# Gate products of a recurrence as three float32r products of high and low parts, in seven of eight blocks

## The chip, the cores and the metric

The kernel runs on one core of a Trainium2 chip. The metric is the device time of one launch in microseconds (us). The program is one long order of instructions on five engines: TensorE (PE, with its weight loads shown apart as PEld), VectorE (DVE), ScalarE (ACT), GpSimd (POOL) and SyncE (SP). Each engine works through its own list strictly in the order in which the program was written, and waits at an instruction until what that instruction needs is there.

## What is computed

Two layers of a transformer-like block. The change lies in layer 0, in its token mixer, a recurrence that runs over the sequence in both directions. For each of 8 blocks of 128 channels, and for each of two directions d, two gates are computed from the convolved input by 128 x 128 matrices, and the scan follows:

```python
r = sigmoid(einsum('blnc,ncd->blnd', xb, wa) + ba)
i = sigmoid(einsum('blnc,ncd->blnd', xb, wi) + bi)
log_a = -RG_C * r * softplus(-lam)
a = exp(log_a)
b = sqrt(-expm1(2.0 * log_a)) * i * xs
a_cum, h = associative_scan(combine, (a, b), axis=1)
```

After the recurrence come its output product, a mixture of experts (32 experts, whose weights stream from HBM), and layer 1 with attention and a second mixture of experts.

## The kernel before

The tokens lie on the free axis: 512 latent tokens, 2 columns of zeros and 256 context tokens, 770 columns (TL), with 128 channels on the partitions. The recurrence runs as a loop over n = 0 to 7 ("block n"). The scheduler is off: every engine does its instructions in the order in which the Python code writes them. In a block:

- TensorE computes zx (`in_mm`, L454: 24 pairs of a 512-column and a 258-column float32r product), then a unit of another, unrelated product (`unit`, L337, named adam), then zg (again 24 pairs), a second unit, the four gate products zr (L1488, plain float32, one for each gate ai and direction d) with a unit behind each direction, and goes on to zx of the next block. Blocks 6 and 7 have no units. zx and zg of block 0 are made before the loop.
- ScalarE copies zx out of PSUM into cb (L1438), applies GELU to zg (L1462, L1463), makes tanh of the four zr (L1490), and then exp, tanh and the square root (L1497 to L1501) for the scan.
- VectorE makes the convolution xc from cb (L1442, L1444), then splits the weights of the next zx into high and low parts (`half_split(0)`, L446 and L447, tile wsx), then does direction 0 of the scan of the block before (`one(0)`, L1398 to L1404), splits the weights of the next zg (`half_split(1)`, tile wsg), does direction 1 of that scan (`one(1)`, L1398 to L1407), and after GpSimd has added both directions (L1410) multiplies the sum with the GELU (L1411, tile yt). The scan of block n is thus done while TensorE is in block n + 1: the list `pend` carries it over.

A float32r product of a and b to nearly float32 accuracy is written in this kernel as three products, high*high, high*low and low*high; `in_mm` does so already. A cast to the type FR gives the high part, and a subtraction the low part.

Of the kernel before, what the change touches and what calls it, by code (L numbers as in the profile page):

```python
# [10 lines left out]
F32 = mybir.dt.float32  # L11
FR = mybir.dt.float32r
BF = mybir.dt.bfloat16
I32 = mybir.dt.int32
AF = mybir.ActivationFunctionType
# [6 lines left out]
P = 128  # L22
D = 1024
KD = D // P
SEQ = 512
CTX = 256
TL = SEQ + 2 + CTX
# [111 lines left out]
def hybrid_kernel(ctx: ExitStack, tc: tile.TileContext, A, out):  # L139
    nc = tc.nc  # L140
    ctx.enter_context(tc.manual_schedule())
    V, SC, PE, GP, SY = nc.vector, nc.scalar, nc.tensor, nc.gpsimd, nc.sync
# [129 lines left out]
    for l in range(2):  # L272
        c_ = cp.tile([P, NEXP], F32, name=f"caps{l}")
        cap = plans[l][1]
        a = 0
        while a < NEXP:
# [4 lines left out]
            a = b  # L281
# [147 lines left out]
    mx = ExitStack()  # L429
    hp = mx.enter_context(tc.tile_pool(name="hp", bufs=1, side="right"))  # L430
    hh = hp.tile([P, KD, TL], FR, name="hh")
    hl = hp.tile([P, KD, TL], FR, name="hl")
# [30 lines left out]
    def tr_tile(nm):  # L463
        return lambda: psa.tile([P, 4, P], F32, tag="tr", name=f"adat{nm}")
# [905 lines left out]
    def y_at(i, a, b):  # L1370
        return yhl[i, a // 2048][:, a % 2048:(b - 1) % 2048 + 1]
# [5 lines left out]
    def y_split(k):  # L1377
        a, b = k * TOK0, (k + 1) * TOK0
        m = min(b, (a // 2048 + 1) * 2048)
        for u, v in ((a, m), (m, b)):  # L1380
            if u < v:
                src = yt_[:, k, u - a:v - a]
                V.tensor_copy(y_at(0, u, v), src)
                V.tensor_sub(y_at(1, u, v), src, y_at(0, u, v).bitcast(F32))

    if True:
        cbs = [mp.tile([P, TL + 3], F32, name=f"cb{i}") for i in range(2)]
        for cb in cbs:
            V.memset(cb[:, 0:2], 0.0)
            V.memset(cb[:, TL + 2:TL + 3], 0.0)  # L1390

        def scans(n, xc, ge, tr, ti, av):

            hs = []

            def one(d):
                a, bb = av[d], tr[d]
                V.scalar_tensor_tensor(ti[d], ti[d], 1.0, xc, op0=OP.add, op1=OP.mult)  # L1398
                V.scalar_tensor_tensor(bb, a, 1.0, bb, op0=OP.add, op1=OP.mult)
                V.scalar_tensor_tensor(bb, bb, 0.5, ti[d], op0=OP.mult, op1=OP.mult)  # L1400
                h = mp.tile([P, SEQ + CTX], F32, tag=f"h{d}", name=f"h{n}_{d}")
                if d == 0:
                    V.tensor_tensor_scan(h[:, SEQ:], a[:, C0:TL], bb[:, C0:TL], 0.0, op0=OP.mult, op1=OP.add)
                    V.tensor_tensor_scan(h[:, 0:SEQ], a[:, 0:SEQ], bb[:, 0:SEQ], h[:, SEQ + CTX - 1:SEQ + CTX], op0=OP.mult, op1=OP.add)  # L1404
                else:
                    V.tensor_tensor_scan(h[:, SEQ:][:, ::-1], a[:, C0:TL][:, ::-1], bb[:, C0:TL][:, ::-1], 0.0, op0=OP.mult, op1=OP.add)
                    V.tensor_tensor_scan(h[:, 0:SEQ][:, ::-1], a[:, 0:SEQ][:, ::-1], bb[:, 0:SEQ][:, ::-1], h[:, SEQ:SEQ + 1], op0=OP.mult, op1=OP.add)  # L1407
                hs.append(h)

            return [lambda: one(0), lambda: one(1), lambda: (V if n == KD - 1 else GP).tensor_add(hs[0], hs[0], hs[1]),  # L1410
                    lambda: V.tensor_mul(yt_[:, n, :], ge, hs[0])]  # L1411

        def half_split(c):

            if split_n[c] % 2 == 0:
                win[c] = S.take()
            w, wi = win[c]
            r = split(w, split_n[c] % 2, f"{'xg'[c]}{split_n[c]}")
            if split_n[c] % 2:
                S.done(wi)  # L1420
            split_n[c] += 1
            return r

        rgws = [load_rgw(0)]
        pend = [lambda: None]
        for n in range(KD):
            i, b = divmod(n, 2)
            cols = None
            if b == 0 and i:
                cols = ada_end(*ada_in_mix[i - 1], aps, *side, tr_tile(f"m{i}"))  # L1430
            if b == 0 and i < 3:
                side = ada_side(*ada_in_mix[i])
            if n + 1 < KD:
                rgws.append(load_rgw(n + 1))
            rgw = rgws[n]
            cb = cbs[n % 2]
            zx = in_mm(*sx, f"x{n}") if n else z0[0]
            SC.activation(cb[:, 2:TL + 2], zx[:, 0:TL], AF.Copy)  # L1438
            if cols:
                cols()  # L1440
            xc = mp.tile([P, TL], F32, tag="xc", name=f"xc{n}", bufs=2)
            V.tensor_scalar(xc, cb[:, 0:TL], prc[:, n:n + 1], prc[:, 32 + n:33 + n], op0=OP.mult, op1=OP.add)  # L1442
            for j in range(1, 4):
                V.scalar_tensor_tensor(xc, cb[:, j:j + TL], prc[:, j * 8 + n:j * 8 + n + 1], xc, op0=OP.mult, op1=OP.add)  # L1444

            if b == 0 and i < 3:
                aps = psa.tile([P, 512], F32, tag="ada", name=f"adam{i}")

            def unit(j):
                if i < 3:  # L1450
                    ada_mm(aps, 4 * b + j)

            unit(0)
            if n + 1 < KD:
                nx = half_split(0)
            else:
                pj = Proj(0, psz, y_cut(0), y_cut(1))
                pj.split(0, ringW, "rw0", SC, GP)
                pend.pop(0)()
            zg = in_mm(*sg, f"g{n}") if n else z0[1]  # L1460
            ge = mp.tile([P, SEQ + CTX], F32, tag="ge", name=f"ge{n}", bufs=2)
            SC.activation(ge[:, 0:SEQ], zg[:, 0:SEQ], AF.Gelu_apprx_tanh)  # L1462
            SC.activation(ge[:, SEQ:], zg[:, C0:TL], AF.Gelu_apprx_tanh)  # L1463
            if n + 1 < KD:
                pend.pop(0)()
                sx, sg = nx, half_split(1)
                while pend:
                    pend.pop(0)()
            else:
                pj.split(1, ringW, "rw0", SC, GP)  # L1470

                mx.close()
                ringE = early.enter_context(tc.tile_pool(name="ringE0", bufs=RE[0], side="right"))
                ph = ExitStack()
                wp = ph.enter_context(tc.tile_pool(name="wp0", bufs=1, side="right"))
                yhl = {(u, c): ringE.tile([P, 2048], FR, tag="re0", name=f"y{'hl'[u]}{c}") for c in (2, 1, 0) for u in range(2)}
                rc, load, shares, shifted, spread = router_consts(0, wp)
                load()
                gate00 = rows_of(0, wp, 0, 1, 0, "gate")
                for k in range(3):  # L1480
                    y_split(k)
            unit(1)
            tr, ti = [], []
            for d in range(2):
                for ai in range(2):
                    z = psz.tile([P, 1024], F32, tag="z", name=f"zr{n}_{d}{ai}")
                    for a, c in ((0, SEQ), (SEQ, TL)):
                        PE.matmul(z[:, a:c], lhsT=rgw[:, ai, d, :], rhs=xc[:, a:c], start=True, stop=True)  # L1488
                    r = mp.tile([P, TL], F32, tag=f"r{ai}{d}", name=f"r{n}_{ai}{d}", bufs=2)
                    SC.activation(r, z[:, 0:TL], AF.Tanh, scale=0.5, bias=hb[:, (ai * 2 + d) * 8 + n:(ai * 2 + d) * 8 + n + 1])  # L1490
                    (ti if ai else tr).append(r)
                unit(2 + d)
            av = []
            for d in range(2):
                a = mp.tile([P, TL], F32, tag=f"a{d}", name=f"a{n}_{d}")
                cidx = d * 8 + n
                SC.activation(a, tr[d], AF.Exp, scale=spm4[:, cidx:cidx + 1], bias=spm4[:, cidx:cidx + 1])  # L1497
                SC.activation(tr[d], tr[d], AF.Tanh, scale=sp2[:, cidx:cidx + 1], bias=sp2[:, cidx:cidx + 1])
                av.append(a)
            for d in range(2):  # L1500
                SC.activation(tr[d], tr[d], AF.Sqrt)  # L1501
            pend += scans(n, xc, ge, tr, ti, av)
# [68 lines left out]
    def part(k):  # L1571
# [5 lines left out]
    side = {  # L1577
        1: lambda: (pre.add(0), pre.square(0, g0)),
        2: lambda: (pre.add(1), pre.half(0, 0)),
        3: lambda: (pre.add(2), part(4), pre.half(0, 1)),  # L1580
        4: lambda: (pre.square(1, g0), pre.mm(0)),
        5: lambda: (pre.square(2, g0), part(3), pre.half(1, 0)),
        6: lambda: (pre.half(1, 1), pre.rstd_a(g0)),
        7: lambda: (pre.rstd_b(g0), pre.norm(0, GP)),
        8: lambda: (part(2), pre.mm(1), pre.half(2, 0)),
# [289 lines left out]
    with tc.tile_pool(name="sp", bufs=1, side="right") as sp_, tc.tile_pool(name="ps", bufs=1, space=PSUM) as pss:  # L1875
# [77 lines left out]
        n = len(units)  # L1953
# [31 lines left out]
    with ExitStack() as ph:  # L1985
# [18 lines left out]
        for k in range(4):  # L2004
# [3 lines left out]
            for t in range(4):  # L2008
                pj.mm(k, t, k == 0, False)
        side = {3: lambda: (pre.gate(3), pre.add(3), pre.square(3, g0)),  # L2010
                4: lambda: shares(psa),
                5: lambda: shifted(),
                6: lambda: spread(psa),
                7: lambda: (pre.gate(0), pre.half(3, 0), pre.add(0), pre.square(0, g0)),
                8: lambda: pre.half(3, 1),
                9: lambda: pre.mm(3),
                10: lambda: pre.half(0, 0),
                11: lambda: (pre.gate(1), pre.half(0, 1), pre.add(1), pre.rstd_a(g0), pre.square(1, g1)),
# [81 lines left out]
```

## Time and profile before

| | |
|---|---|
| median of 3 runs | 1751.87 us (1751.58 to 1751.91) |
| profiled execution, its own time | 1748.35 us |
| its span, first to last instruction | 1746.6 us |
| mean granted TensorE clock | 0.95 |
| loop of the recurrence in the trace | about 66 to 259 us |

The profiled execution is 3.5 us faster than the median, and 1.75 us of its time lie outside its span. In the rows below, "idle before" stands in brackets with what ended it, and rows of the timeline merge neighbours of one line (x8 is eight records). A float32 product appears as two records. A granted clock of 1.00 is 2.4 GHz, 0.50 is 1.2 GHz.

### The profile page before, as it was taken

Reading aid. Unit: us, or ns where it says so; the run is one execution under the profiler, and the core shown is the slowest. Engines: PE = TensorE matmul, PEld = TensorE weight load, DVE = VectorE, ACT = ScalarE, POOL = GpSimd, SP = SyncE. Lnnn points to the kernel's source line nnn. Section 1 sums busy time; section 2 is a strip of 40 time slices with the busy share of each in tenths; the row PEclk is TensorE's granted clock in tenths of the full one; section 3 lists DMA queues with packets and bytes.
Section 4 is the critical chain, followed back from the end, with each engine's and each line's share of the span. In section 5 each row is a group of like instructions: output and inputs, shape, how many; then the busy total and the mean of one; then the engine's idle time right before and its main releaser. Section 6 shows DMA issues by size and latency. Waiting matters only on the chain. (4 is left out here: it accounts for less than half of the span.)

```text
span 1746.6 us, 21397 instructions
## 1 busy us (share of the span) xinstructions
PE 1529.5 (88%) x8096; PEld 774.9 (44%) x8097; DVE 828.0 (47%) x1561; ACT 415.8 (24%) x715; POOL 157.0 (9%) x300
## 2 busy tenths in 40 slices
PE   4999997858899999999788997999499999998877
PEld 1667676742333333333225666777233332432222
DVE  4586779473223224555336557864533333332213
ACT  4545562210000000100005426852110101010000
POOL 0000023231000000111002010011200000000000
PEclk9899999968999999999998998999599999999989
DMA  9565611668999999999993580036499999999996
GB/s 354 210 201 192 244 56 28 225 261 347 362 386 422 422 375 419 419 420 419 420 408 137 217 302 1 1 90 233 181 407 405 413 420 419 420 420 420 420 420 247
DMA packets 100256, 530.99 MB, mean 304 GB/s; under 512 B 10056, under 2 KB 22480, under 8 KB 45872
## 3 DMA queue, kind: packets, MB, share of 16 engines
q1 hardware_dynamic: 85600, 482.43, 69.2%
q0 software_dynamic: 10224, 36.09, 5.8%
q10 hardware_dynamic: 4320, 11.01, 1.8%
q8 instruction: 66, 1.08, 0.3%
q14 instruction: 46, 0.38, 0.1%
HBM read 516.38 MB, written 13.11 MB: 303 GB/s over the span
## 5 line engine op out<-in xcount | busy, mean ns | idle before, releaser
L1021 PE MATMUL G<-w,XT0p 128*32 128x512 f32 (+2 forms) x1312 | 262.2, 603 | 7.9 <-DMA w<-in_moe_w_up_dram 5.0
L1021 PE MATMUL Y<-w,fhs 128*32 128x512 f32 (+2 forms) x1280 | 231.6, 632 | 19.6 <-DMA w<-in_moe_w_down_dram 13.9
L1021 PE MATMUL G<-w,XT1p 128*32 128x512 f32 (+2 forms) x1376 | 230.0, 609 | 15.7 <-DMA w<-in_moe_w_gate_dram 8.0
L1021 PEld LDWEIGHTS G<-w,XT0p 128*32 128x32 f32 (+2 forms) x1312 | 75.6, 128 | 156.0 <-issue 136.8
L1021 PEld LDWEIGHTS Y<-w,fhs 128*32 128x32 f32 (+2 forms) x1280 | 67.4, 127 | 156.8 <-issue 116.8
L1021 PEld LDWEIGHTS G<-w,XT1p 128*32 128x32 f32 (+2 forms) x1376 | 58.6, 119 | 143.1 <-issue 108.1
L1099 DVE TENSOR_TENSOR xs<-xs,cm1p 128x512 f32<-128x512 f32 x112 | 73.4, 684 | 100.7 <-PE cm1p L1097 100.6
L730 POOL DMA_INDIRECT X<-hfd,ix x31 | 30.1, 971 | 661.8 <-PE xt1p L992 294.0
L1099 DVE TENSOR_TENSOR xs<-xs,cm0p 128x512 f32<-128x512 f32 x96 | 63.0, 683 | 42.6 <-PE cm0p L1097 42.0
L1091 ACT ACTIVATE yh<-yt 128x512 fp32r<-128x512 f32 x44 | 27.7, 630 | 225.4 <-DVE yt L1090 225.0
L1044 ACT ACTIVATE ft<-G 128x512 f32<-128x512 f32 x31 | 18.5, 598 | 252.4 <-PE G L1021 252.4
L1090 DVE SCALAR_TENSOR_TENSOR yt<-Y,wn,gf 128x512 f32<-128x512 f32 x28 | 21.0, 751 | 110.3 <-PE Y L1021 105.6
L583 PE MATMUL o<-pw,yh 128*128 128x512 f32 x192 | 65.1, 419 | 7.9 <-DVE pw L571 3.8
L1045 DVE SCALAR_TENSOR_TENSOR ft<-ft,G 128x512 f32<-128x512 f32 x31 | 21.3, 688 | 104.5 <-ACT ft L1044 104.5
L1054 ACT ACTIVATE fhs<-hp 128x512 f32<-128x512 f32 x31 | 18.5, 597 | 186.1 <-PE hp L1053 186.1
L454 PE MATMUL zx<-hh,wsx 128*128 128x512 f32 (+1 forms) x256 | 60.6, 349 | 1.9 <-DVE hh L415 1.8
L454 PE MATMUL zg<-hh,wsg 128*128 128x512 f32 (+1 forms) x256 | 59.2, 344 | 0.0
L1097 PE MATMUL cm1p<-yh,C 128*128 128x512 f32 x112 | 52.5, 469 | 0.6 <-ACT yh L1091 0.4
L1097 PE MATMUL cm0p<-yh,C 128*128 128x512 f32 x96 | 44.6, 464 | 5.7 <-DVE xs L1099 5.0
L1048 DVE SCALAR_TENSOR_TENSOR fh<-ft,G 128x512 f32<-128x512 f32 x31 | 21.3, 687 | 56.4 <-PE G L1021 55.5
L454 PEld LDWEIGHTS zx<-hh,wsx 128*128 128x128 f32 x256 | 40.8, 193 | 13.4 <-issue 5.0
L1488 PE MATMUL zr<-xc,rgw 128*128 128x258 f32 (+1 forms) x128 | 44.9, 496 | 0.9 <-issue 0.9
(428 smaller groups left out, 2482.4 us busy)
## 6 DMA issues: line engine op xcount, KB each, us to landing
w<-in_moe_w_gate_dram SPq DMA_DIRECT2D x128, 1024.0 KB, 16.9
w<-in_moe_w_up_dram SPq DMA_DIRECT2D x128, 1024.0 KB, 17.7
w<-in_moe_w_down_dram SPq DMA_DIRECT2D x128, 1024.0 KB, 19.1
w<-in_ada_w_dram SPq DMA_DIRECT2D x48, 1024.0 KB, 7.0
w<-in_rg_w_in_dram SPq DMA_DIRECT2D x8, 1024.0 KB, 8.2
w<-in_at_w_qkv_dram SPq DMA_DIRECT2D x6, 1024.0 KB, 10.3
kept<-yk ACTq DMA_DIRECT2D x18, 256.0 KB, 7.8
w<-in_rg_w_out_dram SPq DMA_DIRECT2D x4, 1024.0 KB, 4.8
```

Source lines behind the costliest of these rows:

```text
L454: PE.matmul(z[:, a:c], lhsT=lw[:, k, :], rhs=rh[:, k, a:c], start=(k == 0 and i == 0), stop=(k == KD - 1 and i == 2))
L583: PE.matmul(out, lhsT=a(k, t), rhs=b[:, c], start=(start and i == 0), stop=(stop and i == 2))
L730: GP.indirect_dma_start(out=X[0:n, :], out_offset=None, in_=hfd, in_offset=bass.IndirectOffsetOnAxis(ap=idx, axis=0))
L1021: PE.matmul(out[g][a:a + m], lhsT=lhs[:, k, a:a + m], rhs=w[:, at_:at_ + 512], start=(k == 0), stop=(k == last), **at)
L1044: SC.activation(t[0:n], g, AF.Tanh, scale=0.5)
L1045: V.scalar_tensor_tensor(t[0:n], t[0:n], 1.0, g, op0=OP.add, op1=OP.mult)
L1048: (first_half, lambda: V.scalar_tensor_tensor(h_[0:n], t[0:n], 0.5, u, op0=OP.mult, op1=OP.mult)))
L1090: V.scalar_tensor_tensor(yt[0:n], Y[0:n], w[0:n], g[0:n], op0=OP.mult, op1=OP.mult)
L1091: SC.activation(yh_[0:n], yt[0:n], AF.Copy)
L1097: PE.matmul(cm, lhsT=C[0:n, t * P:(t + 1) * P], rhs=y[0:n], start=(i == 0), stop=(i == 1))
L1099: V.tensor_add(a, a, cm)
L1488: PE.matmul(z[:, a:c], lhsT=rgw[:, ai, d, :], rhs=xc[:, a:c], start=True, stop=True)
```

## The change

In blocks 0 to 6 the gate products are no longer one float32 product each. ScalarE copies the gate weights rgw and the convolved input xc to float32r (gh and xh, the high parts). VectorE makes the low part xl of the input right behind the convolution, and the low part gl of the gate weights apart for each direction, at the place in the code where the gate products stand. TensorE then does gh*xh, gh*xl and gl*xh for each half of the columns. Block 7 keeps the float32 product.

```diff
+    rgp = mx.enter_context(tc.tile_pool(name="rgp", bufs=1, side="right"))
...
+            pairs = [(rgw, xc)]
+            if n + 1 < KD:
+                xh, xl = [rgp.tile([P, TL], FR, tag=f"xc{x}", name=f"xc{x}{n}") for x in "hl"]
+                gh = rgp.tile([P, 2, 2, P], FR, tag="rgh", name=f"rgh{n}")
+                SC.activation(gh, rgw, AF.Copy)
+                SC.activation(xh, xc, AF.Copy)
+                V.tensor_sub(xl, xc, xh.bitcast(F32))
+                pairs = [(gh, xh), (gh, xl)]
+
             if b == 0 and i < 3:
...
             unit(1)
             tr, ti = [], []
             for d in range(2):
+                lows = []
+                if len(pairs) > 1:
+                    gl = rgp.tile([P, 2, 1, P], FR, tag="rgl", name=f"rgl{n}{d}")
+                    V.tensor_sub(gl[:, :, 0, :], rgw[:, :, d, :], gh[:, :, d, :].bitcast(F32))
+                    lows = [gl]
                 for ai in range(2):
                     z = psz.tile([P, 1024], F32, tag="z", name=f"zr{n}_{d}{ai}")
                     for a, c in ((0, SEQ), (SEQ, TL)):
-                        PE.matmul(z[:, a:c], lhsT=rgw[:, ai, d, :], rhs=xc[:, a:c], start=True, stop=True)
+                        for u, (lw, rh) in enumerate(pairs):
+                            PE.matmul(z[:, a:c], lhsT=lw[:, ai, d, :], rhs=rh[:, a:c], start=(u == 0), stop=(u + 1 == len(pairs) and not lows))
+                        for gl in lows:
+                            PE.matmul(z[:, a:c], lhsT=gl[:, ai, 0, :], rhs=xh[:, a:c], start=False, stop=True)
```

On TensorE, in block 1, the gate products of direction 0 stood like this before, between two units (adam); zr_00 and zr_01 are the two gates of direction 0:

```order
L337 MATMUL adam_593<-w_637,cl 32x512 x4
L1488 MATMUL zr_00_809<-xc_716,rgw_584 128x512
L1488 MATMUL zr_00_809<-xc_716,rgw_584 128x258
L1488 MATMUL zr_01_814<-xc_716,rgw_584 128x512
L1488 MATMUL zr_01_814<-xc_716,rgw_584 128x258
L337 MATMUL adam_593<-w_653,cl 32x512 x4
```

and with the change like this (xch and xcl are xh and xl, rgh and rgl are gh and gl):

```order
L337 MATMUL adam_602<-w_656,cl 32x512 x4
L1504 MATMUL zr_00_846<-xch_750,rgh_752 128x512
L1504 MATMUL zr_00_846<-xcl_751,rgh_752 128x512
L1506 MATMUL zr_00_846<-xch_750,rgl_844 128x512
L1504 MATMUL zr_00_846<-xch_750,rgh_752 128x258
L1504 MATMUL zr_00_846<-xcl_751,rgh_752 128x258
L1506 MATMUL zr_00_846<-xch_750,rgl_844 128x258
L1504 MATMUL zr_01_855<-xch_750,rgh_752 128x512
L1504 MATMUL zr_01_855<-xcl_751,rgh_752 128x512
L1506 MATMUL zr_01_855<-xch_750,rgl_844 128x512
```

The first product that reads a low part of the weights (rgl) is now the third, and no product behind it can pass it.

On VectorE, the end of block 1 was before: direction 1 of the scan of block 0, the product with the GELU (L1411), and then the work of block 2:

```order
L1400 SCALAR_TENSOR_TENSOR r_01_642<-r_01_642,r_11_647 128x770
L1406 SCALAR_TENSOR_TENSOR h_1_798<-a_1_658,r_01_642 128x256
L1407 SCALAR_TENSOR_TENSOR h_1_798<-a_1_658,h_1_798,r_01_642 128x512
L1411 TENSOR_TENSOR yt__68<-ge_607,h_0_787 128x768
L344 TENSOR_TENSOR adab_579<-adam_593,adab_579 128x512
L363 COPY modc_918<-adatm_913 128x8 x2
L1442 TENSOR_SCALAR xc_921<-cb_570,prc 128x770
```

and is with the change (every line after the inserted ones has a higher number):

```order
L1401 SCALAR_TENSOR_TENSOR r_01_667<-r_01_667,r_11_676 128x770
L1407 SCALAR_TENSOR_TENSOR h_1_833<-a_1_687,r_01_667 128x256
L1408 SCALAR_TENSOR_TENSOR h_1_833<-a_1_687,h_1_833,r_01_667 128x512
L1412 TENSOR_TENSOR yt__68<-ge_616,h_0_822 128x768
L1498 TENSOR_TENSOR rgl_844<-rgw_587,rgh_752 128x256
L1498 TENSOR_TENSOR rgl_870<-rgw_587,rgh_752 128x256
L344 TENSOR_TENSOR adab_582<-adam_602,adab_582 128x512
L363 COPY modc_973<-adatm_968 128x8 x2
L1443 TENSOR_SCALAR xc_976<-cb_573,prc 128x770
L1445 SCALAR_TENSOR_TENSOR xc_976<-cb_573,prc,xc_976 128x770 x3
L1453 TENSOR_TENSOR xcl_982<-xc_976,xch_981 128x770
```

The low parts of the gate weights (rgl) of block 1 stand behind the whole scan of block 0, and the low part of the input (xcl) directly behind the convolution. On ScalarE the start of block 2 is now:

```order
L1439 ACTIVATE cb_573<-zx_918 128x770
L1451 ACTIVATE rgh_983<-rgw_692 128x512
L1452 ACTIVATE xch_981<-xc_976 128x770
L1472 ACT_TABLE_LOAD
L1472 ACTIVATE ge_1050<-zg_1001 128x512
```

where the two copies in the middle are new; the table load and the GELU followed the copy to cb directly before.

## Rows read from the trace of the kernel before

**Rows 1.** The page, parts 1 and 2: busy time; transfer rate in 40 slices.

```profile
PE 1529.5 (88%) x8096; PEld 774.9 (44%) x8097; DVE 828.0 (47%) x1561; ACT 415.8 (24%) x715; POOL 157.0 (9%) x300
...
GB/s 354 210 201 192 244 56 28 225 261 347 362 386 422 422 375 419 419 420 419 420 408 137 217 302 1 1 90 233 181 407 405 413 420 419 420 420 420 420 420 247
```

**Rows 2.** Table of stretches: block 1, and the time behind the loop.

```profile
core 0: us, PE busy (x) PEld busy (x) DVE busy (x) ACT busy (x) POOL busy (x), PEclk, DMA share, GB/s
...
78.00:105.00 27.00, 27.00 (x149) 18.40 (x145) 16.89 (x22) 14.80 (x18) 0.00 (x0) 1.00 0.70 243
...
262.00:300.00 38.00, 31.28 (x154) 24.41 (x152) 36.96 (x40) 10.30 (x11) 10.92 (x5) 0.96 0.07 15
```

**Rows 3.** Timeline of TensorE, block 1: start us, length us, instruction.

```profile
78.01 0.61 PE L454 MATMUL zx<-hh,wsx 128*128 128x512 f32 x2
...
96.39 1.07 PE L337 MATMUL adam<-w,cl 128*32 128x512 f32 x8
97.39 2.85 PE L1488 MATMUL zr<-xc,rgw 128*128 128x512 f32 x8
...
104.94 0.61 PE L454 MATMUL zx<-hh,wsx 128*128 128x512 f32 x2
```

**Rows 4.** Timeline of ScalarE, block 1.

```profile
86.81 0.81 ACT L1438 ACTIVATE cb<-zx 128x770 f32<-128x770 f32 x1 [0.49 <-PE zx L454]
```

**Rows 5.** Timeline of VectorE, block 1: convolution, and end of the chain.

```profile
87.66 0.68 DVE L1442 TENSOR_SCALAR xc<-cb,prc 128x770 f32<-128x770 f32 x1 [13.03 <-ACT cb L1438]
88.37 3.13 DVE L1444 SCALAR_TENSOR_TENSOR xc<-cb,prc,xc 128x770 f32<-128x770 f32 x3
91.42 0.42 DVE L446 CAST wsx<-w 128x512 fp32r<-128x512 f32 x1
...
107.27 0.96 DVE L1411 TENSOR_TENSOR yt__68<-ge,h 128x768 f32<-128x768 f32 x1 [1.97 <-POOL h L1410]
108.15 0.68 DVE L344 TENSOR_TENSOR adab<-adam,adab 128x512 f32<-128x512 f32 x1
```

**Rows 6.** Timeline of block 0: the last weight split on VectorE.

```profile
73.94 0.69 DVE L447 TENSOR_TENSOR wsg<-w,wsg 128x512 fp32r<-128x512 f32 x1
```

**Rows 7.** Timeline of TensorE: gate products of blocks 6 and 7, zg of 7.

```profile
231.11 5.33 PE L1488 MATMUL zr<-xc,rgw 128*128 128x512 f32 x16
236.09 0.70 PE L454 MATMUL zx<-hh,wsx 128*128 128x512 f32 x2
...
244.79 0.52 PE L454 MATMUL zg<-hh,wsg 128*128 128x512 f32 x2
...
253.32 5.33 PE L1488 MATMUL zr<-xc,rgw 128*128 128x512 f32 x16
```

**Rows 8.** Groups by line and shape, 0 to 420 us: busy us, mean ns.

```profile
L1438 ACT ACTIVATE cb<-zx 128x770 f32<-128x770 f32 x8 | 6.5, 810 | 7.8 <-PE zx L454 7.8
...
L416 DVE TENSOR_TENSOR hl<-nth,hh 128x256 fp32r<-128x256 f32 x8 | 3.4, 426 | 0.3
```

**Rows 9.** Table of stretches around idle times of TensorE, columns as in Rows 2.

```profile
41.00:43.00 2.00, 0.00 (x0) 0.00 (x0) 1.93 (x6) 0.00 (x0) 0.00 (x0) 1.00 1.01 414
44.00:46.00 2.00, 1.11 (x4) 0.71 (x4) 0.74 (x5) 0.03 (x1) 0.00 (x0) 0.50 1.00 418
47.00:50.00 3.00, 2.56 (x7) 1.90 (x8) 2.86 (x8) 2.74 (x5) 0.00 (x0) 0.50 1.03 313
50.00:53.00 3.00, 3.00 (x11) 2.54 (x11) 2.90 (x7) 1.35 (x3) 0.00 (x0) 0.50 0.33 86
54.00:57.00 3.00, 3.00 (x18) 2.51 (x18) 2.90 (x8) 2.27 (x4) 0.00 (x0) 1.00 0.00 0
269.00:272.00 3.00, 0.50 (x1) 0.19 (x1) 2.97 (x3) 2.95 (x3) 1.87 (x1) 1.00 0.01 3
272.00:275.00 3.00, 2.99 (x7) 2.41 (x8) 2.97 (x5) 1.63 (x3) 0.89 (x1) 0.50 0.00 0
276.00:279.00 3.00, 3.00 (x15) 2.47 (x14) 2.58 (x3) 1.06 (x1) 1.15 (x1) 1.00 0.00 0
287.00:290.00 3.00, 0.60 (x4) 0.29 (x2) 2.93 (x7) 0.00 (x0) 0.00 (x0) 1.00 0.00 0
```

## The prediction

> **What bounds the kernel now.** I read the page first. TensorE is busy for 88% of the span, twice as long as any other engine [rows 1], so a change in its work counts directly if the stage is its own. The table of stretches says whether it is: in block 1 of the recurrence TensorE is busy for 27.00 of 27 us, VectorE for 16.9, ScalarE for 14.8, at a granted clock of 1.00 [rows 2]. So in this loop TensorE sets the pace, and the others wait for it. Then I read the timeline of a single block, engine by engine, because the new instructions go to all three. A block of TensorE is 26.9 us, from zx at 78.01 to the next zx at 104.94, and the gate products begin at 97.39 [rows 3]. VectorE's list of the same block begins when cb is copied at 86.81 [rows 4] and ends when the instruction behind the product with the GELU starts, at 108.15 [rows 5]. The reader should see the overlap: VectorE's list ends 10.8 us after TensorE has begun the gate products, and 3.2 us after it has left them. That costs nothing now, since nothing that TensorE needs stands at the end of that list.
>
> **The change, part by part.** *Fewer passes on TensorE.* Four float32 gate products take 236.09 - 231.11 = 4.98 us where nothing stands between them [rows 7]. A float32r pair of 512 and 258 columns is what zg is made of: 24 pairs from 244.79 to 253.32, 0.355 us each [rows 7]. The new block has 12 of them, 4.27 us, so 0.71 us less per block and 5.0 us in seven blocks. The Trainium skill (FP8 and Floating Point Precision, section TensorE Precision Notes) counts true float32 as four passes and reduced float32 as one; an estimate by that count is a quarter of the 4.98 us saved, 1.25 us a block. The trace shows less, because a pair has its own cost beside the columns; by the page's count the time predicted below would be nearly 4 us lower.
>
> *The two copies on ScalarE.* The copy of the gate weights waits only for a transfer made a block earlier. The copy of xc takes 0.81 us, by the copy of the same 770 columns to cb [rows 8]; from the square root or a table function it could be 1.0. Both lie in ScalarE's idle time before the GELU. But VectorE's xl stands directly behind xc and waits for that copy.
>
> *xl on VectorE.* A subtraction of this width occupies 0.88 us until the next starts, like the product with the GELU (107.27 to 108.15) [rows 5]. In block 1 the convolution ends at 88.37 + 3.13 = 91.50, where the next instruction had started at 91.42 [rows 5]. Now the copy runs from 91.55 to 92.36, xl starts at 92.41, and the weight split at 93.29: the rest of the list is 1.87 us later.
>
> *gl on VectorE, the part that decides.* The order puts gl behind the scan of the block before and the product with the GELU. TensorE needs it at its third product. With the list moved by 1.87 us, gl starts at 108.15 + 1.87 = 110.02, takes 0.43 us by the subtraction of 256 columns [rows 8], and with 0.05 us for the signal TensorE goes on at 110.50. It came to the gate products at 97.39 and did two 512-column products, 0.47 us (2 x 512/770 of a pair). So it stands idle for about 12.6 us, and behind the waiting product stand all the other gate products, the units and zx of the next block, for which cb and the whole next list of VectorE wait. This idle time isn't hidden by anything: the chain closes on itself.
>
> *The new block.* From zx to cb 86.81 - 78.01 = 8.80 us, from cb to gl 23.69 (110.50 - 86.81), then the rest: 4.27 - 0.47 = 3.80 us of gate products and two units of 1.00 us (96.39 to 97.39) [rows 3]. Together 38.3 us, against 26.9. The second gl reuses the buffer of the first, so it waits for direction 0, but a unit of 1.00 us covers its 0.48 us. Blocks 1 to 5 are of this kind: 5 x 38.3 = 191.5. Block 6 has no units: 36.3 us. Together 227.8 us from zx of block 1 to zx of block 7, where the trace has 236.09 - 78.01 = 158.1: **69.7 us more**. Block 0 has no scan before it: gl stands behind two weight splits, the last of which starts at 73.94 [rows 6] and gives way after 0.61 us, so gl is there at 74.55 + 1.87 + 0.48 = 76.9 (xl some 4.4 us before it: two splits of a 0.42 us and a 0.69 us step, twice each [rows 5, 6]), and zx of block 1 at 76.9 + 5.8 = 82.7 instead of 78.0: **4.7 us more**. Block 7 is unchanged.
>
> *The clock.* After TensorE's idle time from 41 us on, the clock is 0.50 at 44 and still 0.50 from 47 to 53, and 1.00 from 54; after that at 270 it is 0.50 from 272 to 275 and 1.00 from 276 [rows 9]. So after each of the two TensorE ran at 1.2 GHz for 3 to 7 us of work, and lost half of that, 1.5 to 3.5 us. Each of the seven new waits is longer than these. I take 2.4 us each, the middle, **16.8 us** in all; the bounds are 10.5 and 24.5. In the loop this loss is on the path, since the rest of the gate products and zx are what VectorE waits for. The Trainium skill (TensorE: Matmul & The Clock Gate, section HAM oscillation) says that such waits between bursts put the clock down again every time, not once; the two stretches here agree, and a wait of about 2.4 us at 287 us did not do it [rows 9].
>
> *Behind the loop.* The rest moves as a whole. The weights of the experts can't use the time: from 262 to 300 us the DMA share is 0.07 [rows 2], the buffers are full, and the next ones come free by the program's steps after the loop.
>
> *The sum.* 69.7 + 4.7 + 16.8 = 91.2 us; the 5.0 us of fewer passes are in it. From the profiled execution 1748.35 + 91.2 = 1839.6; the median lies 3.5 us above that execution, so for the runs 1751.87 + 91.2 = **1843 us**.
>
> **Rivals.** *Same wait, no loss of clock*: 74.4 us, 1826 us. For it speaks that a short wait at 287 us left the clock at 1.00 [rows 9]; against it that all waits but block 0's (4.4 us) are about 12 us. *The clock stays down longer*, through the units and into zx, because the work after a wait is broken up: up to 5 us lost per wait, 35 in all, 1861 us. For it the 6 to 7 us after 47, where the first products came with gaps; against it the quick return at 276. *A slower copy and a slower list on VectorE* (1.0 us for the copy, contention): 0.3 to 0.5 us per block, 2 to 4 us, inside the range. *The other side: absorbed behind the loop.* If the time of the end were set by the transfer of expert weights, and these ran on during the waits, only the 5.0 us gained on TensorE would be seen: 1747 us. It decides if 91 us of transfers (about 38 MB at the 420 GB/s of the late slices [rows 1]) found buffers in the loop; a DMA share of 0.07 right behind it says that not even a few do [rows 2].
>
> **How the numbers follow.** Forecast as above, 0.78 (1833 to 1854, from the copy's and the clock's bounds); no loss of clock 0.10 (1824 to 1833); longer at the low clock 0.09 (1854 to 1870); absorbed 0.02 (1747); something between 0.01. A measurement of this kernel tells a change from none at about 0.2%, 3.5 us. Faster is the absorbed case, 0.02; the same 0.01; slower 0.97. The forecast's own range leaves out more than 2 in 10, so I reach into both neighbours, from 1828 to 1860.
>
> **What would show it.** In the profile after: a wait of TensorE for VectorE's gl, seven times, one of about 4.4 us and six of about 12 to 14; blocks of 38 to 42 us; a granted clock of 0.50 behind each wait; VectorE's list from cb to gl 23.7 us long without idle time except for the copy and GpSimd's sum; the float32r pairs at 0.355 us at full clock; and the time from the loop's end to the end of the program unchanged. The prediction is wrong if VectorE reaches gl earlier than TensorE, if the waits are much shorter than 12 us, or if the part behind the loop becomes shorter.

## The result: 5.2% slower, by seven waits for a small subtraction

| | before | after |
|---|---|---|
| median of the runs | 1751.72 us (1748.58 to 1751.91, 4 runs) | 1840.89 us (1840.04 to 1845.18, 4 runs) |
| profiled execution, its own time | 1748.35 us | 1840.04 us |
| its span | 1746.6 us | 1838.3 us |
| mean granted TensorE clock | 0.950 | 0.925 |

The time grew to 1.0522 of before, interval 1.0505 to 1.0539: 89 us by the medians, 91.7 us between the two profiled executions. 1843 us had been forecast, with a difference of 91.2 us.

The page of the kernel after, part 1, answers to [rows 1]:

```profile
PE 1542.3 (84%) x8152; PEld 790.5 (43%) x8153; DVE 841.9 (46%) x1582; ACT 425.2 (23%) x729; POOL 155.8 (8%) x300
```

TensorE's busy time grew by only 12.8 us, so nearly all of the loss is time in which TensorE did nothing. The table of waits, TensorE alone, from 60 to 350 us of the kernel after, says for whom it waited (us in total, times, longest):

```profile
PE zr L1506 <- DVE rgl L1498: 79.5, 7, 14.3
PE zr L1504 <- ACT xch L1452: 1.7, 1, 1.7
PE zr L1504 <- DVE xcl L1453: 0.5, 1, 0.5
```

rgl is the low part of the gate weights (gl in the code): seven waits, one for each changed block, 79.5 us. TensorE's timeline of blocks 0, 1 and 6 shows where each stands, and answers to [rows 3] and [rows 7]:

```profile
77.08 0.79 PE L1506 MATMUL zr<-xch,rgl 128*128 128x512 f32 x1 [4.09 <-DVE rgl L1498]
84.88 0.61 PE L454 MATMUL zx<-hh,wsx 128*128 128x512 f32 x2
...
104.27 0.50 PE L1504 MATMUL zr<-xch,rgh 128*128 128x512 f32 x1
104.61 0.40 PE L1504 MATMUL zr<-xcl,rgh 128*128 128x512 f32 x1
117.34 0.79 PE L1506 MATMUL zr<-xch,rgl 128*128 128x512 f32 x1 [12.34 <-DVE rgl L1498]
...
125.47 0.61 PE L454 MATMUL zx<-hh,wsx 128*128 128x512 f32 x2
...
321.55 0.79 PE L1506 MATMUL zr<-xch,rgl 128*128 128x512 f32 x1 [14.33 <-DVE rgl L1498]
327.70 0.51 PE L454 MATMUL zx<-hh,wsx 128*128 128x512 f32 x2
```

In block 1 two products run, and the third, the first to read rgl, comes 12.34 us later. From zx to zx this block takes 125.47 - 84.88 = 40.6 us, against 26.9. The record behind the wait is 0.79 us long; the same 512-column product, when it isn't the first, takes 0.40 us at full clock.

VectorE's timeline of the same block says why rgl is late, and answers to [rows 5]:

```profile
94.54 0.68 DVE L1443 TENSOR_SCALAR xc<-cb,prc 128x770 f32<-128x770 f32 x1 [13.63 <-ACT cb L1439]
95.26 3.13 DVE L1445 SCALAR_TENSOR_TENSOR xc<-cb,prc,xc 128x770 f32<-128x770 f32 x3
99.31 0.96 DVE L1453 TENSOR_TENSOR xcl<-xc,xch 128x770 fp32r<-128x770 f32 x1 [0.92 <-ACT xch L1452]
...
115.99 0.96 DVE L1412 TENSOR_TENSOR yt__68<-ge,h 128x768 f32<-128x768 f32 x1 [1.92 <-POOL h L1411]
116.87 0.42 DVE L1498 TENSOR_TENSOR rgl<-rgw,rgh 128x256 fp32r<-128x256 f32 x1
120.74 0.43 DVE L1498 TENSOR_TENSOR rgl<-rgw,rgh 128x256 fp32r<-128x256 f32 x1 [3.46 <-PE zr L1506]
```

The subtraction is 0.42 us of work. It stands behind the two weight splits and the scan of the block before (from 100.19, where xl gives way, to about 114.1), GpSimd's sum, and the product with the GELU. And the list itself begins only when cb is there (the wait of 13.63 us), which comes from TensorE's zx: so each engine waits for the other once a block. ScalarE's cb starts at 93.70, and TensorE goes on at 117.34, 23.64 us later.

The table of stretches, columns as in [rows 2], shows all of block 1, its part behind the wait, and the time behind the loop:

```profile
85.00:125.00 40.00, 27.66 (x152) 20.27 (x152) 19.88 (x26) 15.55 (x18) 1.80 (x1) 0.83 0.32 107
...
118.00:119.50 1.50, 1.50 (x7) 1.31 (x6) 0.00 (x0) 0.69 (x1) 0.00 (x0) 0.50 0.00 0
120.00:122.00 2.00, 2.00 (x12) 0.60 (x10) 0.43 (x1) 0.90 (x1) 0.00 (x0) 0.55 0.00 0
122.00:125.00 3.00, 3.00 (x24) 2.05 (x20) 0.00 (x0) 1.33 (x2) 0.00 (x0) 1.00 0.57 150
...
345.00:385.00 40.00, 33.62 (x150) 24.77 (x149) 38.94 (x42) 16.77 (x19) 16.92 (x11) 0.91 0.08 17
```

TensorE is busy for 27.7 of 40 us, where it had been busy all the time; behind the wait the granted clock is 0.50 to about 122 us, that is 1.2 GHz for some 4.5 us, and 1.00 again from there. Behind the loop nothing was caught up: from zx of block 7 (327.70) to the profiled execution's end it is 1512.3 us, and it was 1512.3 before (1748.35 - 236.09 [rows 7]). That the two agree so closely is chance: from the start of o, behind the loop, to its end, a profiled execution takes between 1483.5 and 1492.5 us in the ten kernels of this document.

### The profile page after: what moved, and what is told of

Its sections match the earlier page's. It is cut to its first block, busy times and chain, and to the rows that moved or that the text cites. A ratio compares the mean times of both kernels' runs of the same rounds, so it can differ in the third digit from the quotient of the medians.

```text
span 1838.3 us, 21550 instructions
## 1 busy us (share of the span) xinstructions
PE 1542.3 (84%) x8152; PEld 790.5 (43%) x8153; DVE 841.9 (46%) x1582; ACT 425.2 (23%) x729; POOL 155.8 (8%) x300
## 5 line engine op out<-in xcount | busy, mean ns | idle before, releaser
L1506 PE MATMUL zr<-xch,rgl 128*128 128x512 f32 (+1 forms) x56 | 25.6, 457 | 79.5 <-DVE rgl L1498 79.5
L1091 ACT ACTIVATE yh<-yt 128x512 fp32r<-128x512 f32 x44 | 27.7, 630 | 228.0 <-DVE yt L1090 221.3
L1508 ACT ACTIVATE r<-zr,hb 128x770 f32<-128x770 f32 x32 | 28.9, 904 | 114.3 <-PE zr L1506 113.0
L1506 PEld LDWEIGHTS zr<-xch,rgl 128*128 128x128 f32 x56 | 14.5, 258 | 84.0 <-DVE rgl L1498 82.8
L1097 PE MATMUL cm0p<-yh,C 128*128 128x512 f32 x96 | 44.6, 464 | 5.8 <-DVE xs L1099 5.1
## 6 DMA issues: line engine op xcount, KB each, us to landing
w<-in_moe_w_gate_dram SPq DMA_DIRECT2D x128, 1024.0 KB, 19.8
```

The costliest lines, as they stand in the source:

```text
L1091: SC.activation(yh_[0:n], yt[0:n], AF.Copy)
L1097: PE.matmul(cm, lhsT=C[0:n, t * P:(t + 1) * P], rhs=y[0:n], start=(i == 0), stop=(i == 1))
L1506: PE.matmul(z[:, a:c], lhsT=gl[:, ai, 0, :], rhs=xh[:, a:c], start=False, stop=True)
```

## Experiments

Two questions: is the place of gl on VectorE the whole cause, or do the new copies, subtractions and products cost something themselves; and what part is the clock? All kernels start from the changed one, and each is compared with runs of the kernel before on the same chip.

**1. gl early, in all seven blocks.** Both low parts of the weights are made right behind xl, each in a buffer of its own. The space for the second buffer comes from two small temporaries that are reused.

```diff
-        spm4 = cp.tile([P, 16], F32, name="spm4")
-        sp2 = cp.tile([P, 16], F32, name="sp2")
+        spm4, sp2 = sb_, sq_
...
+            def low(d):
+                gl = rgp.tile([P, 2, 1, P], FR, tag=f"rgl{d}", name=f"rgl{n}{d}")
+                V.tensor_sub(gl[:, :, 0, :], rgw[:, :, d, :], gh[:, :, d, :].bitcast(F32))
+                return [gl]
+
+            gls = [low(d) if len(pairs) > 1 else [] for d in range(2)]
...
-                lows = []
-                if len(pairs) > 1:
-                    gl = rgp.tile([P, 2, 1, P], FR, tag="rgl", name=f"rgl{n}{d}")
-                    V.tensor_sub(gl[:, :, 0, :], rgw[:, :, d, :], gh[:, :, d, :].bitcast(F32))
-                    lows = [gl]
+                lows = gls[d]
```

> The two subtractions that make the low parts of the gate weights stand directly behind the low part of the input on VectorE, each into a buffer of its own; everything else is as in the changed kernel. If the place of these subtractions is the cause: no wait of TensorE for them in blocks 1 to 6, 12 pairs of 0.355 us in place of 4.98 us there (0.71 us less per block, 4.3 us), block 0 about 0.8 us longer (its products wait for the copy and two subtractions), so about 1748 us. If the float32r products, the switch between kinds of product, or the added copies and subtractions themselves cost the time, it stays above 1760 us.

Measured: 1749.65 us (1744.41 to 1754.71, 12 runs), before 1749.03 (24 runs), ratio 1.0002 (0.9989 to 1.0015). No wait for rgl is left in the table of waits. So the place of a 0.42 us instruction is the whole loss of 89 us: the same copies, subtractions and products, with gl some 20 instructions earlier, cost nothing in sum. But neither is the gain of some 5 us from fewer passes seen. In the loop it is there: TensorE's timeline of this kernel has

```profile
77.91 0.61 PE L454 MATMUL zx<-hh,wsx 128*128 128x512 f32 x2
...
97.87 0.39 PE L1508 MATMUL zr<-xch,rgl 128*128 128x512 f32 x1
...
103.90 0.61 PE L454 MATMUL zx<-hh,wsx 128*128 128x512 f32 x2
...
226.29 0.39 PE L1506 MATMUL zr<-xch,rgh 128*128 128x512 f32 x1
...
230.50 0.52 PE L454 MATMUL zx<-hh,wsx 128*128 128x512 f32 x2
...
250.33 7.11 PE L1506 MATMUL zr<-xc,rgw 128*128 128x512 f32 x16 [2.68 <-ACT pw L567]
257.77 0.70 PE L582 MATMUL o<-pw,yh 128*128 128x512 f32 x2 [0.33 <-DVE yh L1382]
```

The kernel before has, on ScalarE and on TensorE, for the copy to cb of block 7 and for the first product behind the loop (o, the output product of the recurrence):

```profile
245.81 0.79 ACT L1438 ACTIVATE cb<-zx 128x770 f32<-128x770 f32 x1
```

```profile
259.80 0.70 PE L583 MATMUL o<-pw,yh 128*128 128x512 f32 x2 [1.15 <-DVE yh L1383]
```

From zx of block 1 to zx of block 7 it is 152.6 us, against 158.1 [rows 3, 7]: 5.5 us less. Then block 7 gives most of it back. Its gate products (still float32) come 19.8 us behind its zx, where before they came 253.32 - 236.09 = 17.2 us behind it, and take 7.11 us instead of 5.33 [rows 7]. ScalarE's and VectorE's timelines of the same stretch show the way there:

```profile
238.65 1.03 ACT L1517 ACTIVATE a<-r,sb__197 128x770 f32<-128x770 f32 x1 [3.46 <-DVE h L1407]
...
243.54 0.80 ACT L1438 ACTIVATE cb<-zx 128x770 f32<-128x770 f32 x1
```

```profile
244.37 0.68 DVE L1442 TENSOR_SCALAR xc<-cb,prc 128x770 f32<-128x770 f32 x1 [2.78 <-ACT cb L1438]
245.09 5.14 DVE L1444 SCALAR_TENSOR_TENSOR xc<-cb,prc,xc 128x770 f32<-128x770 f32 x3
```

Block 6 has no units, so it is the shortest block of TensorE. VectorE's list, longer by xl and two gl, no longer fits in it: ScalarE's exp waits 3.46 us for the end of VectorE's scan, and cb of block 7 stands behind it on ScalarE. cb, 9.7 us behind zx before (245.81 - 236.09), is now 13.0 us behind it. The convolution ends at about 250.2, TensorE stands idle for 2.68 us, and its clock falls. (The row names ScalarE's pw as releaser; its copies ended at 245.3 and 249.5, and the product begins 0.1 us behind the convolution, whose result it reads.) By the start of o, at 257.77 instead of 259.80 in the kernel before, 2.0 of the 5.5 us are left. Behind that, this profiled execution takes 1492.5 us, the kernel before 1488.6; as this part differs by several us from profile to profile, and the interval is 0.26% wide (4.6 us), a gain of 2.0 us hardly shows.

**2. The same, with block 0 in float32.** Block 0 has the two small waits for xch and xcl (1.7 and 0.5 us).

```diff
-            if n + 1 < KD:
+            if 0 < n < KD - 1:
```

> As e1_low_early, and block 0 keeps its float32 products as block 7 does, since nothing in block 0 covers the copy and the subtractions. If the place is the cause: 6 x 0.71 us less than before, about 1747.5 us, and 0.8 us less than e1_low_early. If float32r products give nothing in this loop: 1752 us.

Measured: 1748.52 us (12 runs), ratio 0.9992 (0.9979 to 1.0005). Not told apart from before, nor from experiment 1. Block 7's idle time before its gate products is there too (2.67 us), so block 0 wasn't what kept the gain away. Nor was it the fall of the clock in block 7. In experiment 2 TensorE's timeline has

```profile
250.98 5.41 PE L1506 MATMUL zr<-xc,rgw 128*128 128x512 f32 x16 [2.67 <-ACT pw L567]
258.41 0.70 PE L582 MATMUL o<-pw,yh 128*128 128x512 f32 x2 [2.02 <-DVE yh L1382]
```

The clock stays at 1.00 there and the products take 5.41 us, but TensorE then waits 2.02 us for yh, and o comes 27.3 us behind zx of block 7 (231.16), as in experiment 1 (257.77 - 230.50). So it is VectorE's late list that sets the start of o.

**3. Two products instead of three.** gl, its subtraction and its product are left out, xl stays.

```diff
-                if len(pairs) > 1:
-                    gl = rgp.tile([P, 2, 1, P], FR, tag="rgl", name=f"rgl{n}{d}")
-                    V.tensor_sub(gl[:, :, 0, :], rgw[:, :, d, :], gh[:, :, d, :].bitcast(F32))
-                    lows = [gl]
```

> Leaves out the product of the low part of the gate weights and its two subtractions: two float32r products in place of three, so the gates are a little less accurate. If the wait for the low weights is the whole cause and TensorE then sets the pace: 8 pairs, 2.84 us, in place of 4.98 us, 2.1 us less per block in blocks 1 to 6 and about 1 us less in block 0, about 1738 us. If the copies on ScalarE and the subtraction on VectorE cost on the path: between 1745 and 1765 us.

Measured: 1740.56 us (5 runs), ratio 0.9951 (0.9933 to 0.997). Without gl there is no wait for it, and outside block 0, where TensorE waits 1.7 and 0.5 us for xch and xcl, xl with its copy isn't seen to cost anything: block 1 takes 24.6 us from zx to zx (78.90 to 103.45), 2.4 less than before. The give-back in block 7 is here too, and larger: TensorE's timeline has 5.63 us of idle time before these products, and 8.01 us for them:

```profile
248.24 8.01 PE L1500 MATMUL zr<-xc,rgw 128*128 128x512 f32 x16 [5.63 <-issue]
```

**4. The wait kept, the clock kept.** Before the first product that reads rgl, 100 products of 254 columns (32 in block 0) into a part of the PSUM tile that nobody reads keep TensorE at work until gl is there.

```diff
+                        if lows and d == ai == a == 0:
+                            for _ in range(100 if n else 32):
+                                PE.matmul(z[:, TL:1024], lhsT=gh[:, 0, 0, :], rhs=xh[:, 0:1024 - TL], start=True, stop=True)
                         for gl in lows:
```

> The changed kernel, with products that nobody reads (float32r, 254 unused columns of the waiting PSUM tile) in front of the first product that needs a low part: 100 of them in blocks 1 to 6 (about 11.8 us, just under the wait), 32 in block 0. The wait itself stays. If the clock is 1.2 GHz behind each wait because TensorE idled, and that costs 2.4 us a wait: about 1824 us, and a granted clock of 1.00 in the loop. If the waits alone make up the time: 1841 us, or a little more.

Measured: 1826.35 us (1823.64 to 1826.86, 4 runs), ratio 1.0439 (1.0421 to 1.0456). The table of stretches, from just behind block 0's wait to the end of block 1's, and then TensorE's timeline of block 1:

```profile
78.00:117.00 39.00, 38.46 (x257) 31.56 (x256) 19.89 (x26) 16.13 (x18) 1.83 (x1) 1.00 0.45 158
```

```profile
103.61 12.00 PE L1507 MATMUL zr<-xch,rgh 128*128 128x254 f32 x100
116.15 0.50 PE L1509 MATMUL zr<-xch,rgl 128*128 128x512 f32 x1 [0.54 <-DVE rgl L1498]
...
122.29 0.61 PE L454 MATMUL zx<-hh,wsx 128*128 128x512 f32 x2
```

The clock is now 1.00, and from the first product with rgl to the next zx it is 6.14 us instead of 8.13 (125.47 - 117.34). gl doesn't come earlier by that: from zx to its product it is 32.5 us in both kernels (116.15 - 83.65, and 117.34 - 84.88). So of the 89 us some 14.5 by the medians (1840.9 - 1826.35), 12.6 by the two traces up to zx of block 7 (327.70 - 315.08), are the clock, and the rest is the wait as such.

**5. gl late in three blocks only.** As experiment 1, with gl at its late place in blocks 1 to 3.

```diff
+            gls = [low(d) if len(pairs) > 1 and n not in (1, 2, 3) else [] for d in range(2)]
...
+                lows = low(d) if n in (1, 2, 3) else gls[d]
```

> As e1_low_early in blocks 0, 4, 5 and 6; in blocks 1, 2 and 3 the subtractions stand where the change put them. If each late block pays for itself: 3 x (38.3 + 2.4 - 26.2) = 43.5 us above e1_low_early, about 1792 us. If the cost comes once, or is absorbed in the blocks behind: under 1775 us.

Measured: 1790.42 us (4 runs), ratio 1.0238 (1.0219 to 1.0256); three waits, 36.7 us in all, as the table of waits has them:

```profile
PE zr L1508 <- DVE rgl L1457: 36.7, 3, 12.4
```

That is 40.8 us above experiment 1, 13.6 for each late block; by the two traces it is 43.5 us from zx of block 1 to zx of block 7 (274.56 - 78.49, against 230.50 - 77.91). The price is per block and adds up: no single block carries it.

**6. gl behind the first scan.** Both low parts are made behind the split of zg's weights, between the scan's two directions: at a middle place of VectorE's list.

```diff
+            gls = [[], []]
...
                 sx, sg = nx, half_split(1)
+                gls = [low(d) for d in range(2)]
...
+                lows = gls[d]
```

> Both subtractions stand in front of direction 1 of the scan of the block before, behind the second weight split, so about 7.5 us earlier in VectorE's list than in the changed kernel. If the wait is nothing but the place in VectorE's list: waits of about 4.9 us in place of 12.3, 1841 - 6 x 7.45 = about 1796 us with the loss of clock as it was, 1784 us if so short a wait leaves the clock up. If something else holds TensorE: 1841 us.

Measured: 1794.27 us (4 runs), ratio 1.0264 (1.0242 to 1.0286). The table of waits has, for TensorE:

```profile
PE zr L1509 <- DVE rgl L1457: 33.2, 7, 6.6
```

So the wait follows the place: 79.5 us at the end of the list, 33.2 in the middle, none right behind xl. The time above experiment 1 is 44.6 us, more than the waits. By the two traces the stretches behind the seven waits are 14.9 us longer than in experiment 1, 2.1 each, so waits of 4 to 7 us lower the clock too (0.50 from 110 to 113 us, behind the wait of block 1). Against that, block 7 up to o is 4.0 us shorter than in experiment 1 (23.3 us against 27.3): 33.2 + 14.9 - 4.0 is 44.1.

**7. The units first.** The two units that stood behind the gate products are moved ahead of them, so that TensorE has 2 us more to do before it needs gl.

```diff
             unit(1)
+            unit(2)
+            unit(3)
...
-                unit(2 + d)
```

> The changed kernel, with the two units that stood behind the gate products of each direction put in front of all gate products, so that 2 us of TensorE's work are done before the first product that waits. If TensorE can't pass the waiting product: the waits are 2 us shorter in blocks 0 to 5, about 1841 - 12 = 1829 us. If TensorE already passes it, or if the units were not on the path: 1841 us.

Measured: 1825.3 us, a single run. The waits of TensorE, from 47 to 345 us:

```profile
PE zr L1508 <- DVE rgl L1500: 70.5, 6, 15.0
PE adam L337 <- DMA w<-in_ada_w_dram: 3.5, 1, 3.5
```

The units are now done in time in which TensorE would have waited, and no longer stand between gl and the next zx, so the chain gets shorter by them: 15.6 us less than the changed kernel. Block 0 no longer waits for rgl, but the second row is a wait in its place: a unit that comes earlier needs its weights earlier. In block 1 TensorE still waits 11.25 us, 1.1 us less and not 2: it comes to the gate products 1.6 us later behind zx (101.97 - 81.01, against 104.27 - 84.88), and gl comes 0.5 us later, because ScalarE copies cb 9.3 us behind zx (81.01 to 90.31) and not 8.8. The stretch behind the wait is 2.4 us shorter (5.76 us against 8.13), which makes block 1 as a whole 1.9 us shorter. It is a cover, not a cure.

**8. gl early, in blocks 1 to 5.** As experiment 2, and block 6, whose length VectorE's list no longer fits, is left in float32 too. The edit is shown against experiment 2.

```diff
-            if 0 < n < KD - 1:
+            if 0 < n < KD - 2:
```

> As e2_early_not_block0, and block 6 keeps its float32 products too. In the traces of e1 and e2, TensorE's gain of about 5 us in the loop was given back in block 7, where ScalarE's exp for direction 1 waited 3.5 us for VectorE's scan, cb and the convolution of block 7 came late, and TensorE stood idle for 2.7 us in front of the gate products. If VectorE's longer list in block 6, the shortest block, is the cause of that: the wait of ScalarE and the idle time are gone or under 0.5 us, and 5 x 0.71 = 3.5 us stay, about 0.998 of the time before. If the gain is lost to something else: the idle time stays, and the time is that of before or above.

Measured: 1744.45 us (1741.38 to 1747.12, 9 runs), before 1749.54 (14 runs), ratio 0.997 (0.9959 to 0.9982): 5.1 us less, and the fastest version with all three products. TensorE's timeline of this kernel:

```profile
77.80 0.61 PE L454 MATMUL zx<-hh,wsx 128*128 128x512 f32 x2
...
103.77 0.61 PE L454 MATMUL zx<-hh,wsx 128*128 128x512 f32 x2
...
231.14 0.70 PE L454 MATMUL zx<-hh,wsx 128*128 128x512 f32 x2
...
248.34 5.34 PE L1506 MATMUL zr<-xc,rgw 128*128 128x512 f32 x16
254.85 0.70 PE L582 MATMUL o<-pw,yh 128*128 128x512 f32 x2 [1.18 <-DVE yh L1382]
```

Block 7's gate products come 17.2 us behind zx without idle time and take 5.34 us, as before. The lead over the kernel before is 4.95 us at zx of block 7, of which 0.2 us were there before the first changed block (78.01 - 77.80), and still 4.95 at the start of o (259.80 - 254.85). That confirms the account of experiment 1: with five blocks changed instead of seven the kernel is faster, since it is block 6 that makes VectorE late. The intervals of this experiment and of experiment 2 touch; what tells the two apart is the lead at o, 4.95 us here and 1.39 there (259.80 - 258.41).

## Why the prediction was right, point by point

**The place of gl decides: right, and shown.** Experiments 1, 5 and 6 move nothing but gl (all three with its second buffer) and turn the loss off, on in three blocks, and to half.

**The waits: nearly.** "One of about 4.4 us and six of about 12 to 14" were forecast; measured were 4.09, then 12.34, 11.96, 12.40, 11.96, 12.40 and 14.33. From cb to TensorE's going on it is 23.64 us, 23.69 were forecast.

**The sum by the trace.** zx of block 1 stands 6.9 us later than before (84.88 against 78.01), where 4.7 and 2.4 for the clock were forecast. From there to zx of block 7 it is 327.70 - 84.88 = 242.8 us, where 227.8 and six times 2.4, so 242.2, were forecast. Behind that 0.1 us were added, none was forecast. That the sum meets the two profiled executions to 0.5 us (91.2 forecast, 91.7 measured) is in part luck, since the part behind the loop alone varies by more; the medians differ by 89.2 us.

**The clock: right in kind, a little large, by a term next to it.** Measured against the forecast's 5.8 us from the third product to the next zx, the stretches behind the seven waits are 2.0 to 2.6 us longer, 17.0 in all, where 16.8 were forecast. But part of this isn't the clock: at a clock of 1.00 the same stretch takes 6.03 us in experiment 1 (97.87 to 103.90), since products between units take longer than in an unbroken row. Six blocks of that are 1.4 us, which leaves 15.6 for the clock; experiment 4 gave 14.5 by the medians. By its trace it got back 1.2 us in block 0 (zx at 83.65 instead of 84.88) and 11.4 us from there to zx of block 7 (231.4 us instead of 242.8), in six blocks: 2.1 each in blocks 1 to 5, and 0.7 in block 6, where its filler ended 2.5 us early and the clock fell. That is 12.6 us in the loop; what the medians have beyond it isn't seen there. The Trainium skill (TensorE: Matmul & The Clock Gate, section HAM oscillation) had said that each such wait puts the clock down again; all seven did here.

**The gain of fewer passes: mis-sized, and not free.** "0.71 us less per block" came from products that stand in an unbroken row [rows 7]. In block 6 of experiment 1 the measured gain is indeed 4.98 - (230.50 - 226.29) = 0.77 us. In block 1 it is 0.96: 26.93 us from zx to zx before, 25.97 in experiment 8. [rows 3] had that price: 2.78 us from zr to the unit behind it, more than half of 4.98. The prediction's estimate of 1.25 us goes by the four passes that the Trainium skill (FP8 and Floating Point Precision, section TensorE Precision Notes) counts for true float32; the trace has 0.77 to 0.96. The reason that the prediction gives for the difference, a cost of each pair beside its columns, no run here separates. What I hadn't seen is that the gain can be lost at the loop's end.

**The rivals.** No loss of clock (1826 us) and the longer loss (1861 us) both fall: the clock did fall, and was back before the next zx. Where experiment 4 kept the clock in six blocks, it took 1826.35 us. Absorption behind the loop falls: the part behind it has its old length. The slower list on VectorE falls: from cb to gl it was 0.05 us shorter than forecast. For the copy of xc 0.81 us were forecast, and it took 0.85 us.

## What to carry to other kernels

On engines that work in written order, what a new instruction costs is not its length but its place: find what stands before it on its engine, and who waits behind it. 0.42 us of work at the end of a list that itself waits for the consumer cost 13 us a block. And when a change lengthens an engine's list that has room in the usual block, check the shortest block too: here it took back most of the gain of all the others, and with it and block 0 left out the kernel was 5 us faster than before.

## What the hardware showed that I had not expected

- **Three tensor operations on VectorE take 5.14 us instead of 3.13 while GpSimd works.** The convolution's three instructions of 770 columns took 3.13 us in block 1 of the kernel after. In block 7 they took 5.14 in experiment 1, where GpSimd was at work from 245.36 to 248.36, and 5.16 in experiment 8 (242.41 to 247.57), where GpSimd was at work from 242.68 to 245.69. In experiment 1 the scan's first step behind them, 0.95 us in other places, took 3.10 us beside GpSimd's next instruction. The Trainium skill (SBUF — State Buffer, section SBUF: two separate sides) says that VectorE, with two tensor inputs in SBUF, and GpSimd hold a pair of ports for a whole instruction by turns, and that the other is blocked. These times agree: the first of the three instructions had begun before GpSimd's, and the three together lost some 2.0 us beside an instruction of 3.00. That GpSimd is the cause is read from the times alone; no run separates it.
- **A short idle time was enough for the clock in some places, and not in others.** The 2.53 us left in block 6 of experiment 4 and the 2.68 us in block 7 of experiment 1 were each followed by a clock of 0.50 (in the latter, 7.11 us for products of 5.33). At the same place as the latter, 2.67 us in experiment 2 and 2.69 us in experiment 5 left it at 1.00 (5.41 us for the products in both). [rows 9] has both kinds as well: a clock of 0.50 from 272 us, behind a wait of 2.25 us, and one that stayed at 1.00 behind a wait of 2.40 us at 287 us. What tells these cases apart stays open.
- **float32 products cost more beside units**: 2.78 us for the two of a direction, against 2.49 in an unbroken row; for the six float32r pairs 2.29 against 2.10.
